# The low halves of the front's and the queries' weights: a vector subtraction against an adding transfer

## The chip, the cores and the metric

The kernel runs on one core of a Trainium2 chip. The metric is the time of one execution on the device in microseconds (us). The core has a matmul engine (PE, with its weight loads on PEld), a vector engine (DVE), a scalar engine (ACT), GpSimd (POOL) and SyncE (SP, which issues most transfers). All transfers run on 16 DMA engines. Every instruction stream is executed in order on its own engine; semaphores hold an instruction until what it needs has happened.

## The reference

One decoder layer over 1024 tokens with 1024 features:

```python
h = x @ w_in                                   # q | k | v | conv_a | conv_gate
att = sliding_window_attention(rotary(q), rotary(k), v, sinks)
cnv = silu(layer_norm(causal_conv31(conv_a * sigmoid(conv_gate))))
x = layer_norm(alpha * x + concat(att, cnv) @ w_out)
q = x @ w_query                                # 8 heads x 2 halves x 128
top = top16 of q @ sub_keys, then top16 of the 16 x 16 sums, per head
r = alpha * x + sum(gelu(x . u[ids]) * gates * v[ids])      # 128 experts a token
x = layer_norm(r + sigmoid(r @ w_gate) * (p @ w_ple))
```

All of it is float32. A float32 product is made here from three matmuls of rounded (fp32r) operands: high by high, high by low and low by high, where high is the operand rounded to fp32r and low is the operand less its high half.

## The kernel before

The 1024 tokens are cut into 8 tiles of 128: group A has three of them (384 tokens), group B five (640 tokens). The front runs for both groups: x is transposed and split, `s_conv` (streams c0, c1), `s_qkv` (q0, q1), the taps of the convolution (t0, t1, 31 vector instructions a channel block), attention (a0, a1), the convolution's norm (`s_cln`, in l0, l1), the output product `s_wout` (w0, w1), the first layer norm (n0, n1) and the expert queries `s_query` (y for A, and once more for B later). Then group A fetches its 768 rows of expert tables by indirect transfers (`s_gather`, line 775, issued by POOL), while group B does the same sums densely over the whole tables, which takes most of the time: `s_early` (products with u) and `s_dense` (products with v).

The weights of the front and of the queries come through one helper, `w_split` (lines 271 to 277). It is called 76 times, each time for 512 KB: 8 times each for c0 and c1, 6 each for q0 and q1, 8 each for w0 and w1, 16 for y and 16 for the queries of B. In `by_channel` (c, y and the queries) the piece is 1024 x 128, which lands as 8 runs of 512 bytes in each of the 128 partitions; in `by_token` it is 256 x 512 (runs of 2 KB: the last four of q, and w) or 512 x 256 (runs of 1 KB: the first two of q). Below such a call is a set. A set takes three pages, `wraw`, `wh` and `wl`, of a ring of six (`WPAGES`). SP loads `wraw` (line 273), ACT rounds it to `wh` (line 156, called from `split`), DVE subtracts and writes `wl` (line 152), and PE uses both in `mm3` (lines 160 to 162) until the set is done.

What sets the order: PE, ACT, DVE and SP get their order from a scheduler that lists the program on a simulated timeline. POOL alone keeps the order in which the program is written (line 201, `manual_schedule`). The program's order is that of `ORDER` (line 51), a list of streams with so many steps of each, and behind it the two lines that weave the queries of B with gathers:

```python
    weave((s_query(1), 16), (early, UQ), (rows, RQ))     # UQ 9, RQ 105
    weave((s_choose(1), 8 * nB), (early, UC), (rows, RC))  # UC 22, RC 45
```

So a step of the queries of B stands after every six or seven gathers. In the front POOL does the rotary products of attention (lines 370 to 375) and the low halves of the normed convolution (line 481, which is a `split` on POOL; it shows as line 152). In `ORDER` the second step of `s_cln` for group A stands just ahead of the first set of w0. The gathers have seven row buffers (`UB`), which DVE frees (lines 783 and 791), and `s_choose` takes its scratch from the same six pages as the sets.

Of the kernel before, what the change touches and what calls it, by code (L numbers as in the profile page):

```python
# [8 lines left out]
F32 = mybir.dt.float32  # L9
# [4 lines left out]
AF = mybir.ActivationFunctionType  # L14
OP = mybir.AluOpType
# [4 lines left out]
P = 128  # L20
# [78 lines left out]
def layer(tc, io):  # L99
    nc = tc.nc  # L100
# [49 lines left out]
    def sub(eng, o, a, b):  # L150

        return eng.tensor_tensor(o, a, b, op=OP.subtract)  # L152

    def split(hi, lo, src, eng):

        nc.scalar.copy(hi, src)  # L156
        return sub(eng, lo, src, hi.bitcast(F32))
# [30 lines left out]
    def wpage(shape, dt, name):  # L188
        return WP.tile(shape, dt, name=name, tag="wpage", bufs=WPAGES)
# [79 lines left out]
            split(dst[0][:, h:h + 4, sl], dst[1][:, h:h + 4, sl], ps.rearrange("p (k t) -> p k t", k=4), nc.vector)  # L269

    def w_split(src, k, n):
        raw = wpage([P, k, n], F32, "wraw")
        nc.sync.dma_start(raw, src.rearrange("(k p) n -> p k n", p=P))
        hi = wpage([P, k, n], F32R, "wh")
        lo = wpage([P, k, n], F32R, "wl")
        split(hi, lo, raw, nc.vector)
        return hi, lo

    def by_token(gi, src, c0, cn, sink_fn):

        g, (aH, aL) = groups[gi], act[gi]
        pss = [(ph() if j < 4 else pv())[:, :cn] for j in range(len(g))]
        kn = D // cn
        for kq in range(KD // kn):
            wh, wl = w_split(src[P * kn * kq:P * kn * (kq + 1), c0:c0 + cn], kn, cn)
            for j in range(len(g)):
                sl = slice(j * P, (j + 1) * P)
                for k in range(kn):
                    kk = kn * kq + k
                    mm3(pss[j], aH[:, kk, sl], aL[:, kk, sl], wh[:, k, :], wl[:, k, :], kk == 0, kk == KD - 1)  # L290
                if kk == KD - 1:
                    sink_fn(g[j], pss[j])
            yield

    def by_channel(gi, src, c0, sink_fn):

        aH, aL = act[gi]
        wh, wl = w_split(src[:, c0:c0 + P], KD, P)
        for (t0, tn) in n_split(len(groups[gi]) * P):
            ps = ph()[:, :tn]  # L300
            for k in range(KD):
                mm3(ps, wh[:, k, :], wl[:, k, :], aH[:, k, t0:t0 + tn], aL[:, k, t0:t0 + tn], k == 0, k == KD - 1)
            sink_fn(ps, t0, tn)
# [631 lines left out]
    n = len(outs) * len(sets)  # L935
# [115 lines left out]
```

## Time and profile before

| what | value |
|---|---|
| time, median of 3 runs | 2898.01 us (2894.17 to 2898.85) |
| the profiled execution's own time | 2893.7 us |
| its span, first to last instruction | 2891.9 us |
| mean granted clock of PE, share of full | 0.983 |
| PE, DVE, ACT, POOL busy, share of the span | 96%, 83%, 41%, 37% |

The profile is of one execution. "Busy" is the time in which an engine executes; issuing transfers is not counted. A line such as L152 can be that of a helper, so that the tile names tell the use: `wl<-wraw,wh` is the subtraction of `w_split`. An instruction's idle time before it is given with what ended it. The front of both groups takes about the first 500 us of the span, the queries of B run from about 600 to 850, and the dense part fills the rest.

### The profile page before, as it was taken

How to read it: one execution, taken by the hardware profiler on the slowest of the kernel's cores; microseconds unless marked ns; L12 is line 12 of the kernel's file. 1: busy time of each engine (PE TensorE's matmuls, PEld its weight loads, DVE VectorE, ACT ScalarE, POOL GpSimd, SP SyncE). 2: the span in 40 equal slices, each digit the busy share in tenths (PEclk: the TensorE clock that was granted, in tenths of full speed). 3: DMA queues.
4: the chain of work that ended last, by engine and by line, in shares of the span. 5: the costliest groups of instructions: out<-in, count | busy, mean ns of one | idle time of the engine just before them, and what ended most of it. 6: DMA issues, size and time to landing. Idle time of an engine off the chain costs nothing.

```text
span 2891.9 us, 47040 instructions
## 1 busy us (share of the span) xinstructions
PE 2788.4 (96%) x17619; PEld 2511.6 (87%) x17619; DVE 2397.7 (83%) x5137; ACT 1195.6 (41%) x2468; POOL 1071.4 (37%) x851
## 2 busy tenths in 40 slices
PE   8996899999999999999999999999999999999988
PEld 8974589999989999999999999777777777777788
DVE  7999768979999768777888876888888889888865
ACT  4455644533324466667565742222222222222143
POOL 0103010166671035543444443544444455444420
PEclk9997899999999999999999999999999999999999
DMA  5211343499994359998999898999999999999731
GB/s 157 79 52 41 100 122 108 169 379 323 350 326 169 122 218 373 347 347 332 344 330 357 335 359 312 346 339 344 329 353 345 348 365 339 352 348 337 253 108 46
DMA packets 322836, 774.14 MB, mean 268 GB/s; under 512 B 28945, under 2 KB 144145, under 8 KB 320048
## 3 DMA queue, kind: packets, MB, share of 16 engines
q0 software_dynamic: 110592, 402.70, 38.3%
q1 hardware_dynamic: 212016, 368.44, 36.1%
q8 instruction: 138, 2.26, 0.3%
q14 instruction: 90, 0.74, 0.1%
HBM read 681.78 MB, written 89.26 MB: 267 GB/s over the span
## 4 chain that ended last, share of the span: by engine, by line
PE 87%; DVE 9%; issue 1%; DMA 1%; ACT 1%; SPq 0%; POOL 0%; ACTq 0%; DVEq 0%
PE ph L160 15%; PE ph L161 15%; PE ph L162 15%; PE sum L160 7%; PE sum L161 7%; PE sum L162 6%; PE pv L756 4%; PE pt L661 4%; PE part L160 3%; PE part L162 3%; PE part L161 3%; DVE ag L791 1%; PE pt L674 1%; DVE cv L357 1%; DVE row L783 1%
## 5 line engine op out<-in xcount | busy, mean ns | idle before, releaser
L775 POOL DMA_INDIRECT row<-in_peer_v_dram,ids x384 | 513.1, 1336 | 705.6 <-DVE row L783 538.0
L775 POOL DMA_INDIRECT row<-in_peer_u_dram,ids x384 | 491.7, 1281 | 620.9 <-DVE ag L791 312.4
L160 PE MATMUL ph<-acth,uu 128*128 128x320 f32 x2048 | 651.6, 319 | 0.4 <-ACT uu L663 0.2
L161 PE MATMUL ph<-actl,uu 128*128 128x320 f32 x2048 | 636.7, 311 | 0.2 <-issue 0.2
L162 PE MATMUL ph<-acth,uu 128*128 128x320 f32 x2048 | 635.1, 311 | 0.0
L791 DVE SCALAR_TENSOR_TENSOR ag<-row,hb,ag 128x1024 f32<-128x1024 f32 x384 | 491.4, 1280 | 2.8 <-issue 1.3
L783 DVE SCALAR_TENSOR_TENSOR row<-row,x 128x1024 f32<-128x1024 f32 x384 | 466.8, 1219 | 6.6 <-DMA row<-in_peer_u_dram,ids 6.0
L161 PEld LDWEIGHTS ph<-actl,uu 128*128 128x128 f32 x2048 | 387.1, 189 | 1.2
L160 PEld LDWEIGHTS ph<-acth,uu 128*128 128x128 f32 x2048 | 386.4, 189 | 1.7 <-ACT uu L663 0.5
L162 PEld LDWEIGHTS ph<-acth,uu 128*128 128x128 f32 x2048 | 385.5, 189 | 1.0 <-issue 0.5
L161 PE MATMUL sum<-vl,ah 128*128 128x512 f32 x896 | 350.9, 398 | 0.0
L160 PE MATMUL sum<-vh,ah 128*128 128x512 f32 x896 | 337.0, 399 | 1.3 <-ACT vh L156 0.9
L156 ACT CAST ah<-ge 128x640 fp32r<-128x640 f32 x128 | 92.9, 728 | 562.1 <-DVE ge L870 336.5
L162 PE MATMUL sum<-vh,al 128*128 128x512 f32 x896 | 291.9, 396 | 0.0
L750 ACT ACTIVATE o<-oo,rest 128x128 bf16<-128x128 bf16 x640 | 196.7, 392 | 30.6 <-DVE oo L745 25.9
L160 PEld LDWEIGHTS sum<-vh,ah 128*128 128x128 f32 x896 | 169.6, 189 | 44.3 <-ACT vh L156 1.7
L161 PEld LDWEIGHTS sum<-vl,ah 128*128 128x128 f32 x896 | 169.6, 189 | 41.3
L162 PEld LDWEIGHTS sum<-vh,al 128*128 128x128 f32 x896 | 168.7, 188 | 41.2
L663 ACT CAST uu<-pt 128x512 fp32r<-128x512 f32 x256 | 150.8, 592 | 120.8 <-PE pt L661 111.5
L701 ACT ACTIVATE ge<-ph 128x320 f32<-128x320 f32 x256 | 108.7, 437 | 217.7 <-PE ph L162 183.7
L152 DVE TENSOR_TENSOR vl<-raw,vh 128x1024 fp32r<-128x1024 f32 x128 | 153.9, 1219 | 27.2 <-ACT vh L156 27.1
L160 PE MATMUL part<-vh,ah 128*128 128x512 f32 x384 | 155.0, 404 | 21.8 <-DVE acc L918 13.7
(300 smaller groups left out, 5592.6 us busy)
## 6 DMA issues: line engine op xcount, KB each, us to landing
raw<-in_peer_v_dram SPq DMA_DIRECT2D x128, 512.0 KB
raw<-in_peer_u_dram SPq DMA_DIRECT2D x81, 512.0 KB
g_dr<-stage SPq DMA_DIRECT2D x20, 2048.0 KB
gt<-g_dr SPq DMA_DIRECT2D x21, 1920.0 KB
e_dr<-ge SPq DMA_DIRECT2D x122, 320.0 KB
ge<-e_dr SPq DMA_DIRECT2D x122, 320.0 KB
uraw<-in_peer_u_dram SPq DMA_DIRECT2D x47, 512.0 KB
wraw<-in_peer_query_dram SPq DMA_DIRECT2D x32, 512.0 KB
```

What stands on the lines that cost most here:

```text
L152: return eng.tensor_tensor(o, a, b, op=OP.subtract)
L160: nc.tensor.matmul(ps, lh, rh, start=first, stop=False)
L161: nc.tensor.matmul(ps, lh, rl, start=False, stop=False)
L162: nc.tensor.matmul(ps, ll, rh, start=False, stop=last)
L661: nc.tensor.matmul(ps[:, k * P:(k + 1) * P], raws[c][:, (4 * h + k) * P:(4 * h + k + 1) * P], ident, is_transpose=True, start=k == 0, stop ...
L663: nc.scalar.copy(uu[:, 0], turned)
L701: nc.scalar.activation(ge[:, c0:c0 + cn], o, AF.Gelu)
L750: nc.scalar.mul(o2[:, 2, e], oo[:, 1, e], rest[:, t + e:t + e + 1])
L756: nc.tensor.matmul(ps[:, e * P:(e + 1) * P], o2[:, m, 4 * f4 + e], oo[:, 0, 4 * f4 + e], start=m == 0, stop=m == 2)
L775: nc.gpsimd.indirect_dma_start(out=t, out_offset=None, in_=table, in_offset=bass.IndirectOffsetOnAxis(ap=ids[i][:, s:s + 1], axis=0))
L783: behind(nc.vector.scalar_tensor_tensor(u, u, 1.0, x1, op0=OP.mult, op1=OP.mult, accum_out=hb[:, e:e + 1]), marks, TIE)
L791: behind(nc.vector.scalar_tensor_tensor(ag, v, blocks[b][:, e:e + 1], ag, op0=OP.mult, op1=OP.add), marks, TIE)
```

## The change

`w_split` no longer subtracts on DVE. ACT still rounds `wraw` to `wh`. ACT then writes the negative of `wh` to `wl`, and a transfer issued by POOL reads the weights from memory a second time and adds them onto `wl`. The three pages, the load by SP and the products stay as they are. `split` is used elsewhere as before.

```diff
     def w_split(src, k, n):
+        src = src.rearrange("(k p) n -> p k n", p=P)
         raw = wpage([P, k, n], F32, "wraw")
-        nc.sync.dma_start(raw, src.rearrange("(k p) n -> p k n", p=P))
+        nc.sync.dma_start(raw, src)
         hi = wpage([P, k, n], F32R, "wh")
         lo = wpage([P, k, n], F32R, "wl")
-        split(hi, lo, raw, nc.vector)
+        nc.scalar.copy(hi, raw)
+
+        nc.scalar.activation(lo, hi.bitcast(F32), AF.Copy, scale=-1.0)
+        nc.gpsimd.dma_start(lo, src, accum_op=OP.add)
         return hi, lo
```

## Rows read from the trace of the kernel before

**Rows 1.** The page, busy time and share of the span of each engine

```profile
PE 2788.4 (96%) x17619; PEld 2511.6 (87%) x17619; DVE 2397.7 (83%) x5137; ACT 1195.6 (41%) x2468; POOL 1071.4 (37%) x851
```

**Rows 2.** Stretches: busy us (count) of PE, PEld, DVE, ACT, POOL; clock, DMA share, GB/s

```profile
17.00:82.00 65.00, 65.00 (x378) 61.49 (x377) 57.19 (x102) 26.70 (x39) 1.06 (x2) 1.00 0.47 139
82.00:199.00 117.00, 117.00 (x774) 105.81 (x773) 112.46 (x193) 57.04 (x128) 15.43 (x23) 1.00 0.22 64
...
217.00:276.00 59.00, 34.94 (x186) 25.05 (x184) 59.00 (x85) 29.48 (x72) 23.47 (x28) 0.80 0.14 45
276.00:357.00 81.00, 67.23 (x321) 45.68 (x321) 60.20 (x112) 51.19 (x132) 0.00 (x0) 0.78 0.27 91
357.00:446.00 89.00, 89.00 (x444) 77.90 (x443) 56.64 (x190) 36.38 (x60) 7.26 (x8) 1.00 0.40 121
446.00:501.00 55.00, 53.04 (x333) 52.06 (x332) 52.73 (x183) 26.21 (x51) 0.00 (x0) 1.00 0.31 91
...
625.00:846.00 221.00, 212.82 (x1440) 208.26 (x1439) 209.71 (x639) 68.57 (x145) 152.73 (x106) 0.96 0.96 334
846.00:1000.00 154.00, 154.00 (x1075) 151.59 (x1075) 145.89 (x920) 70.36 (x133) 25.61 (x19) 1.00 0.49 178
```

**Rows 3.** Chain of waits between 199 and 357 us, its shares by line

```profile
by line: DVE cv L357 18.7%; PE pv L432 8.5%; PE pt L428 7.4%; PE pt L396 6.9%; PE ph L160 4.8%; PE ph L161 4.3%; PE ph L162 4.2%; DVE sc L400 4.2%; issue 3.7%; DMA xc<-in_x_dram 3.6%; DVE st L406 3.6%; PE pv L464 3.2%; DVE wl L152 2.9%; ACT
```

**Rows 4.** Stretches, tile `wl` alone: PE, PEld, DVE, POOL busy us (count)

```profile
82.00:217.00 135.00, 70.64 (x217) 40.71 (x216) 18.67 (x15) 0.00 (x0) 1.00 0.20 59
217.00:276.00 59.00, 9.43 (x20) 4.57 (x20) 4.96 (x4) 0.00 (x0) 0.80 0.14 45
```

**Rows 5.** Instructions by tile: count, duration min/median/max in ns, first and last start

```profile
L152 DVE TENSOR_TENSOR wl<-wraw,wh x76: 1199/1222/1876, 14.7 to 811.5; 128x1024 fp32r<-128x1024 f32 x76
...
L770 ACT ACTIVATE ag<-x x3: 1055/1073/1074, 504.6 to 2032.7; 128x1024 f32<-128x1024 f32 x3
```

**Rows 6.** Timeline: start us, duration us, engine, line; sets of c0

```profile
33.01 0.34 PE L162 MATMUL ph<-actah,wl 128*128 128x384 f32 x1
...
33.38 0.37 SPq L273 DMA_DIRECT2D wraw<-in_w_in_dram  x1
...
37.33 1.05 ACT L156 CAST wh<-wraw 128x1024 fp32r<-128x1024 f32 x1 [1.48 <-DMA wraw<-in_w_in_dram]
...
39.00 0.42 PE L162 MATMUL ph<-actah,wl 128*128 128x384 f32 x1
...
43.68 0.42 PE L162 MATMUL ph<-actah,wl 128*128 128x384 f32 x1
```

**Rows 7.** Timeline, sets of y: first use of `wl` in y6 and y15

```profile
446.40 0.34 PE L162 MATMUL ph<-actah,wl 128*128 128x384 f32 x1
...
494.72 0.34 PE L162 MATMUL ph<-actah,wl 128*128 128x384 f32 x1
```

**Rows 8.** Timeline of POOL: a short gather and a long one

```profile
558.29 0.94 POOL L775 DMA_INDIRECT row<-in_peer_u_dram,ids  x1 [0.30 <-issue]
...
668.15 3.08 POOL L775 DMA_INDIRECT row<-in_peer_v_dram,ids  x1 [0.30 <-DVE top L532]
```

**Rows 9.** First set of B's queries (SP's load, ACT's cast), and gathers before that load

```profile
594.70 0.39 SPq L273 DMA_DIRECT2D wraw<-in_peer_query_dram  x1
...
612.02 1.05 ACT L156 CAST wh<-wraw 128x1024 fp32r<-128x1024 f32 x1 [2.19 <-DMA wraw<-in_peer_query_dram]
...
556.00:594.70 38.70, 27.80 (x22) 1.00 0.93 346
```

**Rows 10.** Timeline: w0's first `wl` on PE, group A's norm on POOL

```profile
199.16 0.39 PE L161 MATMUL ph<-wl,actah 128*128 128x512 f32 x1
...
234.56 2.29 POOL L152 TENSOR_TENSOR actal<-cv,actah 128x384 fp32r<-128x384 f32 x2 [65.76 <-ACT actah L156]
```

## The prediction

> **What bounds the kernel now.** I read the busy shares first: PE 96%, DVE 83%, ACT 41%, POOL 37% [rows 1]. The share of PE over the whole span says only that most of it is bound by products; the 76 sets all lie before 850 us, so I read the stretches of that part next [rows 2]. Three kinds are to be seen. From 17 to 199 us PE is busy all the time, 65.0 of 65 and 117.0 of 117 us. From 217 to 276 DVE is busy for 59.0 of 59 us and PE for 34.9, at a clock of 0.80: there DVE sets the pace, and PE still idles to 357 (67.2 of 81). From 357 on PE is full again (89.0 of 89, 53.0 of 55, 212.8 of 221, 154 of 154). The chain of waits between 199 and 357 agrees: its largest share is DVE's taps, 18.7%, and the subtraction of `w_split` is on it by itself with 2.9% of 158 us, 4.6 us [rows 3]. So time that DVE is spared before 276 us can shorten the kernel; later PE would have to be given time, and a later low half takes it away.
>
> **What goes.** 76 subtractions of 1.22 us leave DVE [rows 5], 93 us in all. Only those ahead of the DVE-bound stretch or in it count: 15 between 82 and 217 (18.7 us) and 4 between 217 and 276 (5.0 us) [rows 4], together 23.7 us, since DVE is busy 112.5 of 117 us and then 59 of 59 there [rows 2]. I take them in full as -23.7; the other end is -4.6, what the chain itself holds. The first 14 lie in a stretch where PE is the bound, the rest behind 357 us.
>
> **What ACT gets.** 76 negations. A scaled copy of 128x1024 takes 1.07 us [rows 5]; ACT is busy 26.7 of 65 and 57.0 of 117 us in the dense stretches [rows 2], so the 1.07 us matters only as latency ahead of the transfer, in the sum below.
>
> **What the new transfer costs.** The low half now waits for ACT's negation, POOL's issue and a landing. No accumulating transfer is in this trace, so I bound the wait A from the negation's end to the landing. A plain load of a set takes 3.95 us from SP's issue (33.38) to the cast (37.33) [rows 6]. Between 446 and 501 us the 16 DMA engines move 91 GB/s at a share of 0.31, that is 294 GB/s when busy, so one pass over 512 KB is 1.8 us of all of them [rows 2]. An adding transfer reads `wl` too, and for the second operand I add one such pass: 3.95 + 1.8 = 5.75; with that read hidden it is 3.95. POOL's issue: the shortest gather, of 128 pieces, holds POOL for 0.94 us [rows 8]. If that price is fixed, A has 0.94; if it goes by pieces, a set of 1024 pieces has 8 x 0.94 = 7.5. Nothing shows which, and the row has a piece count and not a split of its time, so I take the middle in ratio, 2.65 (for sets of 2 KB runs with 256 pieces, 1.3). So A is 4.9 to 13.2 us, taken as 8.4 (by_channel) and 7.2 (the six sets of q0, two of them with 1 KB runs).
>
> **How the latency becomes time.** Six pages hold three sets in flight: SP issues a load (33.38) as soon as the third set before it has left PE (last matmul 33.01 + 0.34) [rows 6]. A set then needs 3.95 load + 1.05 cast + 1.07 negation + A + its own time on PE, 4.7 us (39.00 to 43.68) [rows 6], and three sets share that. Before, with 1.22 for DVE in place of 1.07 + A, it is (3.95 + 1.05 + 1.22 + 4.7) / 3 = 3.6, under the 4.7 that PE takes: hidden. After it is (10.8 + A) / 3.
> - c0, 8 sets: 19.2 / 3 = 6.4 against 4.7, +1.7 each, +13.6. q0, 6 sets: 18.0 / 3 = 6.0, +1.3 each, +7.8. Together +21.4 in a stretch where PE is the bound.
> - c1 and q1: 14 sets fill 117 us [rows 2], 8.4 each; (6.1 + 8.4 + 8.4) / 3 = 7.6 is less, so 0. PE is the cover; with A at 13.2 it would be +0.8 for each of the eight of c1.
> - w0: POOL keeps its written order, so its first low halves wait behind group A's norm, which ran on POOL at 234.6, though PE used the first one at 199.2 [rows 10]. About 9 us of product move from 199 to behind 240. PE idles 24 us between 217 and 276 [rows 2] and takes them: 0. The rotary products behind these issues wait too; attention waits for DVE there anyway.
> - w1 fills 357 to 446 with y0 to y5: (89 - 6 x 5.4) / 8 = 7.1 us a set; A for 2 KB runs is near 7.1, (6.1 + 7.1 + 7.1) / 3 = 6.8 is less: 0 for w1.
> - y: from y6 to y15 a set takes (494.72 - 446.40) / 9 = 5.4 us [rows 7]; after it is 6.4, +1.0 for 14 sets (y2 to y15), +14. PE is full from there to the end, so nothing gives it back.
>
> **The queries of B.** Here POOL's order costs most. The first low half stands behind three gathers and ahead of all others; its load was issued at 594.7 and cast at 612.0, and 22 gathers had been issued before 594.7 [rows 9]. Those now wait, and at each later step six or seven gathers wait for the set's negation, which waits for a page and so for PE. Their vector work, 22 x 1.2 us, moves back into a stretch where DVE is busy 209.7 of 221; the 16 subtractions that leave it give 19.5 us in return [rows 2, 5]. The DMA engines are at 0.96 there, and 16 adding transfers bring 16 x 3.6 = 58 us of their time; but gathers pushed behind 846 find a share of 0.49 and only 19 others [rows 2]. Ends: -8 (PE's idle time there goes) and +58; I take +10, near the lower end, since what is pushed out has room.
>
> **Sum:** -23.7 + 21.4 + 14 + 10 = +22 us. The profiled execution took 2893.7 (span 2891.9 and 1.8 around it); so 2916. The median of the runs is 4.3 above that execution, so I forecast 2920. A difference under 0.2% (5.8 us) can't be told from none by a measurement of this kernel.
>
> **Rivals.**
> 1. *The transfer is short and DVE's relief decides* (not slower). POOL's issue is a fixed 0.94 and the second read is hidden: A = 4.9. Then c0 and q0 cost (15.7 / 3 - 4.7) x 14 = +7, y nothing (5.2 under 5.4), the queries of B -8: -23.7 + 7 - 8 = -24, 2874. For it: sets are read by pieces as large as before, and SP's issue is 0.37 [rows 6]. Against it: the transfer reads twice. It decides where 14 x (2 x (10.8 + A) / 3 - 10.1) falls under 23.7, at A under 6.9.
> 2. *POOL pays by the piece.* A = 13.2 for 1024 pieces: c0 +26, q0 +10, c1 +7, y +37, the queries +45 (POOL gets 16 x 7.5 = 120 us beside 152.7 of 221 busy [rows 2]), -24: +101, 2999. For it: the pieces are eight times a gather's. Against it: a gather also reads an index for each piece.
> 3. *DVE's work lengthens POOL's issue.* Gathers take from 0.94 to 3.08 us, the long one begun while DVE was at L532 [rows 8]. If each issue pays those 2.1 us, 28 sets (c0, q0, y) cost 0.7 more each: +20 on the forecast, 2940. The Trainium skill, SBUF — State Buffer, section "SBUF: two separate sides", warns of this: descriptors for POOL's transfers are written through a port that some vector instructions hold. By that rule the change puts 76 transfers on the path that suffers; the spread of the gathers agrees, though it doesn't show the cause.
> 4. *The waits change places:* DVE's relief and PE's stalls cancel. With A near 6.9 the sum is within 5.8 us of nothing, 2898.
>
> That the change doesn't do what it says is no case: the subtraction is one instruction of DVE, and it is gone.
>
> **How the numbers follow.** Forecast 0.40 (2908 to 2935), rival 1 0.20, rival 2 0.13, rival 3 0.12, rival 4 0.15. Slower: 0.40 + 0.13 + 0.12 and a little of rival 4, 0.67. Faster: most of rival 1, 0.18. Same: 0.15. The range goes from just below rival 1 to just short of rival 2's full price, 2870 to 2990, which leaves out under 2 in 10.
>
> **What would show it.** In the profile after: DVE without L152 on `wl`; PE waiting for a DMA on `wl` in 17 to 82 and 446 to 501, with c0's sets at 6.4 us instead of 4.7; the 217 to 276 stretch shorter; POOL's rows for the new transfer near 2.7 us (0.94 speaks for rival 1, 7 for rival 2, a wide spread for rival 3); few gathers before the first set of B's queries. I am wrong if sets of c0 still take 4.7 us, or if the time before 357 us shrinks by more than the y sets and the queries of B give back.

## The result and the profile after

The changed kernel took 2961.49 us (median of 4 runs, 2959.06 to 2967.38) against 2896.09 us for the kernel before, a ratio of 1.0228 with a 95% interval of 1.0213 to 1.0243. That is 65 us slower, where +22 was forecast: the sign held, and the range (2870 to 2990) held the time, but the size was nearly three times the sum. The profiled execution took 2959.06 us with a span of 2957.3, against 2891.9 before, so it shows the same 65.4 us.

The page after has the busy times, the packets of POOL's queue (number, MB, share of 16 engines) and the shares of the chain that ended last; [rows 1] answer to the first line.

```profile
PE 2801.6 (95%) x17619; PEld 2517.6 (85%) x17619; DVE 2318.0 (78%) x5061; ACT 1268.1 (43%) x2543; POOL 1144.2 (39%) x927
...
q0 software_dynamic: 169152, 442.55, 47.2%
...
PE 68%; DMA 12%; DVE 11%; issue 6%; ACT 3%; POOL 1%; SPq 0%; DVEq 0%; POOLq 0%; ACTq 0%
```

The same lines of the page of before:

```profile
q0 software_dynamic: 110592, 402.70, 38.3%
...
PE 87%; DVE 9%; issue 1%; DMA 1%; ACT 1%; SPq 0%; POOL 0%; ACTq 0%; DVEq 0%
```

DVE has 79.7 us less to do (the 76 subtractions are 94 us; its other instructions took some 14 us more) and ACT 72.5 more. The chain tells the rest: transfers were 1% of it and are now 12%. POOL's queue took 0.472 x 2957.3 - 0.383 x 2891.9 = 288 us more of all 16 engines, 3.8 us for each of the 76 sets.

Stretches of the trace after (columns as in [rows 2], to which they answer; the marks are moved to the same sets):

```profile
17.00:117.00 100.00, 75.67 (x376) 67.14 (x377) 66.41 (x133) 42.07 (x55) 21.31 (x15) 0.88 0.88 168
117.00:248.00 131.00, 129.12 (x839) 112.69 (x838) 102.77 (x170) 77.37 (x164) 29.49 (x37) 1.00 0.59 114
248.00:310.00 62.00, 37.45 (x182) 27.72 (x180) 51.43 (x75) 34.89 (x72) 23.35 (x29) 0.78 0.53 110
310.00:392.00 82.00, 64.81 (x333) 43.43 (x333) 45.39 (x95) 55.98 (x141) 8.01 (x10) 0.85 0.46 110
392.00:495.00 103.00, 92.75 (x442) 79.48 (x443) 41.00 (x177) 48.69 (x73) 22.55 (x20) 0.97 0.73 158
495.00:567.00 72.00, 59.24 (x347) 56.59 (x346) 50.53 (x221) 37.62 (x65) 13.99 (x9) 0.93 0.87 155
...
687.00:912.00 225.00, 216.74 (x1494) 213.25 (x1493) 190.01 (x699) 81.36 (x164) 124.35 (x104) 0.98 1.04 324
```

The first stretch does in 100 us what took 65, the fifth in 72 what took 55, and in both the DMA engines are near full (0.88 and 0.87 where it was 0.47 and 0.31). What PE waits for in 0 to 117, 248 to 392 and 392 to 570 us (us in total, times, longest):

```profile
PE ph L161 <- DMA wl<-in_w_in_dram: 9.0, 2, 6.5
PE ph L162 <- DMA wl<-in_w_in_dram: 7.3, 4, 3.0
...
PE ph L161 <- DMA wl<-in_w_out_dram: 28.7, 5, 17.8
...
PE ph L162 <- DMA wl<-in_peer_query_dram: 14.9, 8, 5.1
```

To place the 65 us I cut both traces at the end of the last high-by-high product (line 160) of five sets, so that each stretch holds the same products. The forecast is the prediction's sum, sorted into the same stretches (its queries of B into the last but one).

| stretch, us | before | after | change | forecast |
|---|---|---|---|---|
| start to the first set of c0 | 22.8 | 32.1 | +9.3 | 0 |
| from there to the last set of q0 | 59.3 | 84.9 | +25.6 | +21.4 |
| to the first set of y (c1, q1, attention A, w0) | 278.3 | 279.1 | +0.8 | -23.7 |
| to the last set of y (w1 and y) | 139.8 | 171.1 | +31.3 | +14 |
| to the last set of B's queries | 345.8 | 344.5 | -1.3 | +10 |
| to the end | 2045.9 | 2045.6 | -0.3 | 0 |
| sum | 2891.9 | 2957.3 | +65.4 | +22 |

The new instructions, by tile (count, min/median/max in ns, first and last start; then the time from issue to landing in us):

```profile
L280 POOL DMA_DIRECT2D wl<-in_peer_query_dram x32: 1540/1622/1730, 338.2 to 888.8; - x32
L280 POOL DMA_DIRECT2D wl<-in_w_in_dram x28: 1187/1546/1827, 16.7 to 217.8; - x28
L280 POOL DMA_DIRECT2D wl<-in_w_out_dram x16: 1188/1203/1696, 262.4 to 479.1; - x16
...
L279 ACT ACTIVATE wl<-wh x76: 1039/1060/1093, 15.3 to 884.7; 128x1024 fp32r<-128x1024 f32 x76
...
DMA to landing us min/median/max: 5.9/7.4/16.3
```

### The profile page after: what moved, and what is told of

The parts are those of the page before. It is cut to its first block, busy times and chain, and to the rows that moved or that the text cites. A ratio compares the mean times of both kernels' runs of the same rounds, so it can differ in the third digit from the quotient of the medians.

```text
span 2957.3 us, 47285 instructions
## 1 busy us (share of the span) xinstructions
PE 2801.6 (95%) x17619; PEld 2517.6 (85%) x17619; DVE 2318.0 (78%) x5061; ACT 1268.1 (43%) x2543; POOL 1144.2 (39%) x927
## 4 chain that ended last, share of the span: by engine, by line
PE 68%; DMA 12%; DVE 11%; issue 6%; ACT 3%; POOL 1%; SPq 0%; DVEq 0%; POOLq 0%; ACTq 0%
PE ph L161 11%; PE ph L162 11%; PE ph L160 11%; PE sum L161 6%; PE sum L160 6%; PE sum L162 6%; PE pv L760 3%; PE pt L665 3%; PE part L160 3%; PE part L161 2%; PE part L162 2%; DVE ag L795 2%; DVE row L787 2%; DMA wl<-in_peer_query_dram 2%; DMA wraw<-in_w_in_dram 2%
## 5 line engine op out<-in xcount | busy, mean ns | idle before, releaser
L779 POOL DMA_INDIRECT row<-in_peer_v_dram,ids x384 | 495.5, 1290 | 628.2 <-DVE row L787 451.2
L779 POOL DMA_INDIRECT row<-in_peer_u_dram,ids x384 | 483.1, 1258 | 522.4 <-DVE ag L795 322.0
L160 PE MATMUL sum<-vh,ah 128*128 128x512 f32 x896 | 344.4, 399 | 1.3 <-ACT ah L156 1.3
```

Of the source, the lines that this page charges most:

```text
L160: nc.tensor.matmul(ps, lh, rh, start=first, stop=False)
L779: nc.gpsimd.indirect_dma_start(out=t, out_offset=None, in_=table, in_offset=bass.IndirectOffsetOnAxis(ap=ids[i][:, s:s + 1], axis=0))
```

## The experiments

Differences in us are medians less the median of the kernel before on the same chip; changes by stretch come from one profiled execution each. In the stretch behind the queries of B, in which `w_split` has no part, single executions lie between -4 and +12 us, also for a control whose median does not move (norm_dve_before, +8.5). I read nothing from that stretch.

**One part at a time.** `w_split` gets a flag; without it a set is made as before. Six kernels, each with another line for which sets are new:

```diff
+    def w_split(src, k, n, new):
         raw = wpage([P, k, n], F32, "wraw")
         ...
+        if not new:
+            split(hi, lo, raw, nc.vector)
+            return hi, lo
         nc.scalar.copy(hi, raw)
...
+    def adds(gi, src):
+        return src is w_in and gi == 0     # only_c0q0
```

In the others the line is `src is w_in and gi == 1` (only_c1q1), `src is w_out and gi == 0` (only_w0), `src is w_q and gi == 0` (only_y), `src is w_out and gi == 1` (only_w1) and `src is w_q and gi == 1` (only_qb).

> The adding transfer only for the 14 sets of group A's convolution and q, k, v (c0, q0); the other 62 sets subtract on DVE as before. Latency (the low half is late in a ring of six pages, and PE has no cover here): these sets end some 35 us later, as in the full change (117.2 against 82.3 us), and the total is 20 to 35 us over the kernel before. POOL's order (time is lost only where POOL's written order holds an issue): nothing stands ahead of these sets on POOL, so 0 to 3 us. Bytes (each second read slows the rest, 65 us / 76 sets = 0.86 us a set): 12 us.

> The adding transfer only for the 14 sets of c1 and q1, which PE consumes in 8 us each. Latency: hidden, and DVE is spared 14 x 1.22 = 17 us ahead of the stretch that it bounds, so 5 to 17 us under the kernel before. POOL's order: the rotary products stand behind some of these issues, 0 to 5 us over. Bytes: 12 us over.

> The adding transfer only for the eight sets of group A's output product (w0). POOL's order: the first issue waits behind the low halves of group A's norm, PE stands still for it as in the full change (17.8 us), 10 to 18 us over the kernel before. Latency alone: eight sets at about 1 us more, partly in PE's idle time, 0 to 6 us. Bytes: 7 us.

> The adding transfer only for the 16 sets of group A's queries (y). Latency: y6 to y15 go from 5.4 to 6.9 us a set, and with y2 to y5 the total is 18 to 25 us over the kernel before. POOL's order: nothing long stands ahead of them on POOL, 0 to 5 us. Bytes: 14 us.

> The adding transfer only for the eight sets of w1. As predicted: 0. As the full change's trace reads (w1's end moves 6.6 us more than the end of y5): 3 to 10 us over the kernel before.

> The adding transfer only for the 16 sets of the queries of B, between the gathers. As predicted: +10 us (POOL's order holds gathers, the DMA engines are full). As the full change's trace reads (from the first to the last set 217.6 us against 214.0 before, and 6 us won back behind): within 6 us of the kernel before.

Measured, with the change of each stretch of the table above:

| kernel | ratio (95%) | us | first set | c0, q0 | to y | w1, y | to B's last |
|---|---|---|---|---|---|---|---|
| only_c0q0 | 1.0101 (1.0084 to 1.0119) | +27 | +10.2 | +26.2 | -6.3 | -0.9 | -0.8 |
| only_c1q1 | 1.0037 (1.0023 to 1.0051) | +8 | -0.3 | 0.0 | +2.9 | -0.4 | +0.7 |
| only_w0 | 1.0078 (1.0058 to 1.0098) | +22 | +0.7 | 0.0 | +22.7 | -0.2 | +1.6 |
| only_y | 1.0104 (1.0084 to 1.0124) | +27 | -0.2 | 0.0 | +0.8 | +21.0 | -1.1 |
| only_w1 | 1.0034 (1.0023 to 1.0046) | +11 | +0.9 | +0.1 | +3.6 | +12.3 | +3.2 |
| only_qb | 1.0002 (0.9991 to 1.0014) | 0 | +0.9 | 0.0 | +3.1 | -0.6 | -0.2 |

The losses of the whole change are reproduced where they arise: the first set and c0/q0 by the first kernel (+36.4, and +34.9 in the whole change), the stretch of w1 and y by two (21.0 + 12.3, and +31.3). Only the stretch to y doesn't add up: the five parts have +24 there, the whole +0.8. What PE waits for, in only_w0 between 199 and 360 us and in only_y between 360 and 525:

```profile
PE ph L161 <- DMA wl<-in_w_out_dram: 35.6, 4, 21.7
```

```profile
PE ph L162 <- DMA wl<-in_peer_query_dram: 12.5, 7, 3.6
```

What follows: c0/q0, w0, y and w1 each cost by themselves; the queries of B cost nothing by themselves, though I had put +10 on them; c1 and q1 cost little on their path (PE waited 3.8 us for their `wl`) but returned none of the vector time that they save (+8, where 5 to 17 us less was expected if DVE's relief counts).

**What DVE's relief is worth.** The negation stays, the transfer goes; the low half is then only the negative of the high half.

```diff
         nc.scalar.activation(lo, hi.bitcast(F32), AF.Copy, scale=-1.0)
-        nc.gpsimd.dma_start(lo, src, accum_op=OP.add)
```

> All 76 sets are rounded and negated by ACT as in the change, and no transfer follows: the weights are not added, so the low half is the negative of the high one. It has all of DVE's relief and ACT's added work and none of the transfer. If DVE's relief was worth what the prediction said, 20 to 24 us under the kernel before; if DVE's time was not what held the stretch from 217 to 357 us, within 6 us of the kernel before, and the whole loss of the change is then the transfer's.

Measured: 0.9885 (0.9866 to 0.9904), -33 us, more than the 20 to 24 expected. By stretch -0.1, +4.1, -23.3, -1.8 and -17.7. Its windows of c1 and q1, and where [rows 2] have 34.94 of 59 and 67.23 of 81 for PE:

```profile
86.00:215.00 129.00, 129.00 (x839) 113.03 (x838) 114.07 (x193) 79.10 (x166) 23.30 (x24) 1.00 0.21 62
...
217.00:276.00 59.00, 50.83 (x247) 35.19 (x245) 54.98 (x87) 41.76 (x96) 21.78 (x28) 0.83 0.19 63
276.00:357.00 81.00, 70.80 (x376) 53.32 (x376) 48.41 (x128) 61.19 (x139) 3.41 (x4) 0.89 0.32 103
```

PE does 50.8 us of work where it did 34.9. So the relief of all 76 sets is worth 23.3 us ahead of y, the size that the prediction took, and another 17.7 in the stretch with the queries of B, where it had at most 8. The transfer itself then costs 33 + 65 = 98 us.

That the 23.3 come from the 19 subtractions which the prediction counted is not shown. 13 of them are those of c1 and q1 and 6 those of w0. only_c1q1 takes the 13 away: the last tap of the convolution then ends at 291.8 us in place of 307.7, yet w0's last low product starts at 314.8, as late as before (312.2); in relief_all it starts at 293.9. PE's wait for the cast of a set of w0 goes the same way (from 199 us to 360 in before, to 363 in only_c1q1, to 341 in relief_all):

```profile
PE ph L160 <- ACT wh L156: 9.1, 2, 8.6
...
PE ph L160 <- ACT wh L156: 8.2, 1, 8.2
...
PE ph L160 <- ACT wh L277: 0.2, 1, 0.2
```

So w0's own subtractions are the likelier place; no run takes them alone away without a transfer.

**Which part of the transfer.** Two kernels keep every instruction and every wait; like relief_all they don't compute the reference. The first adds only the first slab of a set (64 KB of a 1024 x 128 piece, 128 or 256 KB of the others); the second moves all of it but overwrites.

```diff
-        nc.gpsimd.dma_start(lo, src, accum_op=OP.add)
+        nc.gpsimd.dma_start(lo[:, :1, :], src[:, :1, :], accum_op=OP.add)   # small_add
+        nc.gpsimd.dma_start(lo, src)                                        # plain_pool
```

> The change, with the adding transfer for the first slab of each set alone (an eighth of the bytes for by_channel, a quarter or half for by_token), so the other slabs hold the negative of the high half. Issue, completion, POOL's order and every wait stay; the transfer's time on the DMA engines nearly goes. If the engines' time sets the pace: 2864 (all transfers gone) and w0's wait of at most 18 us, so 2866 to 2884. If fixed latency in the ring sets it (landing still 5 to 6 us): (10.8 + 5.5) / 3 = 5.4 us a set of the first 14 against 4.55, +12, y within 2 us, so 2884 to 2900.

> The change with a transfer on POOL that writes the weights over the negated half instead of adding them, so the low half holds the weights themselves; the same bytes are read from memory, nothing is read from the page. If the adding makes the transfer slow, its landing falls from 7.4 us to some 5.5 and the total by (1.9 / 3) x 28 = 18 us and w0's share; if issue, fetch and completion are the most of it, landing and total stay within 1 us and 6 us.

Measured: small_add 0.9978 (0.9963 to 0.9992), -5 us; plain_pool 1.0041 (1.0027 to 1.0055), +12 us. By tile, small_add's issues and landings, and plain_pool's issues:

```profile
L280 POOL DMA_DIRECT2D wl<-in_peer_query_dram x32: 853/928/1025, 301.6 to 816.1; - x32
...
DMA to landing us min/median/max: 2.5/4.1/10.0
```

```profile
L280 POOL DMA_DIRECT2D wl<-in_peer_query_dram x32: 876/927/952, 309.6 to 835.3; - x32
L280 POOL DMA_DIRECT2D wl<-in_w_in_dram x28: 698/876/1076, 17.0 to 200.1; - x28
L280 POOL DMA_DIRECT2D wl<-in_w_out_dram x16: 698/716/757, 244.9 to 441.1; - x16
```

The 98 us fall into three steps: -33 without a transfer, -5 with a short one (28 us for POOL's order, its issue, a short landing and an eighth to a half of the bytes), +12 with the whole 512 KB (17 us for bytes), +65 with the adding (53 us, far more than the 18 us and w0's share that were expected of it). About half of the price is the adding: it lengthens the issue from 0.93 to 1.62 us for 1024 pieces and the time on the DMA engines. Queues by packets, MB and share of 16 engines: after in 17 to 117 us, plain_pool in 17 to 100, before in 17 to 82:

```profile
q0 software_dynamic: 11295, 7.77, 57.1%
q1 hardware_dynamic: 11796, 8.98, 30.3%
```

```profile
q0 software_dynamic: 10652, 7.44, 44.9%
```

```profile
q1 hardware_dynamic: 11777, 8.96, 46.5%
```

An adding set of 0.524 MB takes 57.1 us x 0.524 / 7.77 = 3.85 us of all engines, an overwriting one 0.449 x 83 x 0.524 / 7.44 = 2.62, and SP's load of the same bytes 0.465 x 65 x 0.524 / 8.96 = 1.77. These windows hold pieces of 512 bytes to 2 KB. Over the whole run POOL's queue moves the same packets and bytes when it overwrites, at a share of 0.452 of 2908.0 us:

```profile
q0 software_dynamic: 169152, 442.55, 45.2%
```

That is 207 us over before, 2.7 us a set against 3.8 with the adding. For y alone, all of it in pieces of 512 bytes, an adding set takes 0.575 x 67 x 0.524 / 4.73 = 4.3 us (500 to 567 us of after) and an overwriting one 0.537 x 61 x 0.524 / 4.98 = 3.4 (455 to 516 us of plain_pool). So the adding costs 1.2 to 1.5 overwriting transfers of POOL and in c0 and q0 2.2 of SP's loads. The Trainium skill, Collectives: The Full Stack, section "The bandwidth ceiling: the fold count and why AG ≠ RS ≠ AR", puts the price of the add in a collective down to its two source reads; carried over to this transfer, which is an estimate, that would give about 2. That lies between the two; the runs don't show which base is fair, since POOL's overwriting transfer also turns float32 into fp32r and SP's load does not.

**How many sets are in flight.** One page more (with one taken from another ring, so that it fits) or one less, with the change and without it:

```diff
-PAGES, WPAGES, RAWS, GEB, OB = 5, 6, 3, 3, 2
+PAGES, WPAGES, RAWS, GEB, OB = 4, 7, 3, 3, 2     # ring7, ring7_before
+PAGES, WPAGES, RAWS, GEB, OB = 5, 5, 3, 3, 2     # ring5, ring5_before
```

> The change with seven pages for the sets instead of six, the room taken from the other ring (four pages instead of five). Latency: 3.5 sets in flight instead of three, so a set of c0 or y takes (10.8 + 7.4) / 3.5 = 5.2 us instead of 6.1 or more, some 25 us off the change's 2961 if the smaller ring costs nothing. POOL's order and bytes: no gain.

> The kernel before with seven pages for the sets and four in the other ring, the control of that step. Latency: the sets of before are hidden with six pages, so nothing is gained, 0 to 10 us over the kernel before for the smaller other ring; the gain of the seventh page is then the change's alone. If it gains some 30 us here too, the ring and not the transfer's latency was what the step showed.

> The change with five pages for the sets instead of six. Latency: 2.5 sets in flight instead of three, (10.8 + 7.4) / 2.5 = 7.3 us a set of c0, q0 and y against 6.5, 20 to 35 us over the change's 2961. Engines' time: the pace is held by 6.1 us a set whatever the ring, within 8 us of 2961.

> The kernel before with five pages, the control of that step. Latency: 10.9 / 2.5 = 4.4 us a set is still under PE's 4.55 to 4.7, so 0 to 10 us over the kernel before.

| pages | with the change | without | what the change costs | c0/q0, us a set with the change |
|---|---|---|---|---|
| 7 | 1.0103 (1.0081 to 1.0126), +32 | 1.0042 (1.0026 to 1.0058), +12 | 20 | 72.3 / 13 = 5.56 |
| 6 | 1.0228 (1.0213 to 1.0243), +65 | the kernel before | 65 | 84.9 / 13 = 6.53 |
| 5 | 1.0358 (1.0340 to 1.0375), +107 | 1.0093 (1.0075 to 1.0111), +31 | 76 | 97.1 / 13 = 7.47 |

The last column follows the sets in flight. In the changed kernel a set needs its page for `wraw` only until the cast, so two pages a set count. In the trace after the sixth load of c0 is issued at 46.6 us, when the third set before it has left PE (46.7), and its last low product ends at 66.8: three sets share these 20.2 us, 6.7 each. The landings between 17 and 117 us (the last number, median in us):

```profile
wl<-in_w_in_dram POOLq DMA_DIRECT2D x15, 512.0 KB, 6.8
wraw<-in_w_in_dram SPq DMA_DIRECT2D x14, 512.0 KB, 5.4
```

With 5.4 for `wraw`, 1.05 cast, 1.06 negation, 0.3 to POOL's issue, 6.8 from there to the landing of `wl` and 4.7 on PE, a set takes 19.3 us; over 3.5, 3 and 2.5 sets in flight that is 5.5, 6.4 and 7.7, against 5.56, 6.53 and 7.47. The landings are those of six pages. With each run's own (4.2 and 6.6 us with seven pages, 4.0 and 6.5 with five) the sums are 5.1 and 7.0: the order holds, the size to half a us. The kernel before lost 6.9 us to the fifth page there (66.2 for the 13 sets, 5.1 each in place of 4.56), where its sum had none. So in c0 and q0 latency through the pages decides. The seventh page ends the gain, since the DMA engines are then full, at a share of 0.97 in ring7, and 3.85 + 1.77 = 5.6 us of them for a set are what was measured:

```profile
17.00:104.00 87.00, 71.15 (x371) 63.80 (x371) 65.30 (x132) 40.50 (x53) 21.52 (x15) 0.94 0.97 192
```

The control with five pages cost more than expected, +31, part of it in w1 and y (+11.9). So the whole change does not follow the page count as well as this one stretch: from six to five it lost only 11 us more than its control.

**w0 behind the norm.** The trace after, POOL and then PE (start, duration, and the idle time before with what ended it):

```profile
257.75 4.68 POOL L152 TENSOR_TENSOR actal<-cv,actah 128x384 fp32r<-128x384 f32 x4 [38.35 <-ACT actah L156]
262.38 2.42 POOL L280 DMA_DIRECT2D wl<-in_w_out_dram  x2
```

```profile
268.53 0.79 PE L161 MATMUL ph<-wl,actah 128*128 128x512 f32 x1 [17.78 <-DMA wl<-in_w_out_dram]
```

POOL stands for 38 us at group A's norm, the first two transfers of w0 are issued behind it, and PE stands 17.8 us. Then the norm's low halves of group A were moved to DVE, with the change and without it:

```diff
-                split(aH[:, 4 + b, sl], aL[:, 4 + b, sl], c[:, b, sl], nc.gpsimd)
+                split(aH[:, 4 + b, sl], aL[:, 4 + b, sl], c[:, b, sl], nc.gpsimd if gi else nc.vector)
```

> The change, with the low halves of group A's normed convolution (four instructions) on DVE instead of POOL, so that nothing long stands ahead of w0's first issue on POOL. POOL's order: the wait of 17.8 us for w0's first low half goes and the total falls by 10 to 20 us, to some 2943 to 2952. Latency (w0's delay lies in parallel with that of the first 14 sets): 0 to 6 us off.

> The kernel before with the same move of four instructions from POOL to DVE, as the control of that step. 0 to 5 us from the kernel before by either theory: 4 x 0.5 us more on DVE.

Measured: 1.0189 (1.0171 to 1.0207) and 0.9995 (0.9985 to 1.0005): +56 us with the change, -2 without. PE's wait on these transfers between 248 and 392 us falls from 28.7 to 11.1 us, the longest from 17.8 to 2.9:

```profile
PE ph L161 <- DMA wl<-in_w_out_dram: 11.1, 5, 2.9
```

The stretch to y is 11.4 us shorter than with the change as it was (-10.6 in place of +0.8), of which 6.0 are lost again in w1 and y. So the hold behind the norm is real, and is worth about 10 us in the end (+56 against +65).

**The subtraction on POOL instead.** For the 52 sets of c, q, y and w1 `split` runs on POOL with no second transfer:

```diff
-        split(hi, lo, raw, nc.vector)
+        split(hi, lo, raw, nc.gpsimd)
```

> No transfer: the subtraction itself runs on POOL instead of DVE for 52 sets (all but w0 and the queries of B). DVE gets its relief in the front, and the low half comes some 2.3 us after the cast instead of 1.2 (128x2560 takes 5.7 us on POOL). If latency is what costs, the sets still hide it ((3.95 + 1.05 + 2.3 + 4.7) / 3 = 4.0 under 4.7) and the total is 8 to 20 us under the kernel before; if POOL's order or a share of the port with DVE costs more, 0 to 15 us over.

Measured: 1.0168 (1.0147 to 1.0189), +49 us, outside both expectations; c0 and q0 have +37.8 of it, and there PE waited 25.4 us for two subtractions. By tile, and on the timeline of POOL, DVE and PE:

```profile
L152 POOL TENSOR_TENSOR wl<-wraw,wh x55: 2352/2414/18417, 14.5 to 2842.7; 128x1024 fp32r<-128x1024 f32 x52, 128x2560 fp32r<-128x2560 f32 x3
```

```profile
69.43 18.42 POOL L152 TENSOR_TENSOR wl<-wraw,wh 128x1024 fp32r<-128x1024 f32 x1 [4.25 <-PE ph L162]
...
94.25 15.88 POOL L152 TENSOR_TENSOR wl<-wraw,wh 128x1024 fp32r<-128x1024 f32 x1 [2.62 <-issue]
```

```profile
66.53 19.13 DVE L364 SCALAR_TENSOR_TENSOR cv<-hc,cw,cv 128x384 f32<-128x384 f32 x36
...
91.98 15.95 DVE L364 SCALAR_TENSOR_TENSOR cv<-hc,cw,cv 128x384 f32<-128x384 f32 x30
```

```profile
87.90 0.80 PE L161 MATMUL ph<-wl,actah 128*128 128x512 f32 x1 [13.99 <-POOL wl L152]
```

A subtraction takes 2.4 us on POOL, but the two that met an unbroken run of DVE's taps (36 and 30 of them) ended only some 2 us after it. It is no way out here. Of the versions that compute the reference none is measurably faster than the kernel before.

## Why the prediction was wrong, and what of it held

The forecast of +22 had the direction and missed the size at three terms of its sum. The stretch with w0 was to give back 23.7 us, with w0's late low halves at 0, and gave +0.8. w1 at 0 and y at +14 came to +31.3. The first set, at 0, cost 9.3. Against that the queries of B cost 11 less than forecast.

**What bounds each stretch: right.** PE's full stretches at 17 to 82 and 446 to 501 us [rows 2] were where a later low half became time, and six pages were the means. The forecast of 6.4 and 6.0 us a set for c0 and q0 averages 6.2; measured 6.53. A was taken as 8.4 us and 0.3 + 6.8 = 7.1 was measured; in return `wraw` took 5.4 us to land beside the adding transfers, where [rows 6] gave 3.95. The two misses nearly cancel, which is luck; the term stands (+21.4 against +25.6).

**The first set: a term that was not in the sum, +9.3.** The sum counted sets in a steady row, three in flight. No earlier set covers the first: its transfer was issued at 16.7 and its first low product ran at 27.5.

**w0 at nothing: the step that failed worst.** The text saw that w0's first low halves would stand behind the norm [rows 10], but let PE's 24 idle us of 217 to 276 take the 9 us of product. PE takes its instructions in order, so idle time that lies behind a waiting matmul can't be filled with it or with anything after it. The stall of 17.8 us on PE and 28.7 in all falls into just the stretch in which DVE's relief should have appeared; by itself w0 costs 22.7 us there (only_w0). So the relief, -23.7 in the sum and 23.3 in relief_all, does not show: DVE idles there instead (51.4 of 62 us busy, where [rows 2] has 59.0 of 59). The match of 23.7 and 23.3 may be luck, since 13 of the 19 subtractions behind it gave nothing in only_c1q1. Here the prediction named the wait, but not what stands behind it on PE.

**c1 and q1 at nothing: about right.** PE is busy 129.1 of the 131 us between 117 and 248 us after the change. Their last set ends later because work from behind has moved ahead of it: in relief_all, without any transfer, the stretch holds 129 us of PE in 129, and 839 products as here, where [rows 2] has 774. But the relief that was counted for these sets did not come: only_c1q1 had its taps done 16 us earlier and was still +2.9 us at y. Its path there runs through w0, as read above; what holds w0 stays open.

**w1 at nothing and y at +14: too low, +31.3 in the trace.** Cut once more, the 31.3 are 7.3 for y1 to y5, 6.6 for w1, 7.0 from w1's last set to y6 and 10.4 for y7 to y15. The 7.0 belong to y6: only_y, where w1 is as before, has 5.1 there, and only_w1 has 0. So y's sets cost 24.7 us, 1.6 each in place of +1.0 (y7 to y15 take 60.5 / 9 = 6.7 us each, and 5.6 before between the same marks). Why they take more than the 6.4 of the sum stays open. The granted clock in 495 to 567 us is 0.93 where it was 1.00, but it can hardly be the main cause: only_y loses 8.6 us in y7 to y15, against the 10.4, at 0.97.

```profile
454.00:522.00 68.00, 57.34 (x345) 54.52 (x344) 50.65 (x223) 36.47 (x63) 14.00 (x9) 0.97 0.87 159
```

The 6.6 of w1 were counted at nothing; alone it costs 12.3. There the cover was 0.3 us a set (6.8 against 7.1), from a mean that took in work that is not w1's: before, its sets follow each other every 6.8 us, so there was none.

**The DMA engines: sized, but set against nothing.** The prediction had 16 x 3.6 us for the transfers of B's queries, and 3.85 a set was measured. It did not set the 3.6 beside PE's time in the front: with 1.8 for the load that is 5.4 us of all engines for a set that PE does in 4.6. Six pages hid this floor, since latency asked for more; seven pages ran into it.

**The queries of B at +10: wrong, 0.** Alone they cost nothing (0.9991 to 1.0014). The gathers did move (the first from 556.5 to 616.7 us), but the stretch has 216.7 of 225 us of PE as before, and what the transfer costs there is about what DVE's relief brings (17.7 us without the transfer, 1.3 with it). The vector work that moves back leaves DVE at 190 of 225 us, under the 209.7 of 221 of before [rows 2], and did not stand in PE's way.

**The rivals.** Rival 1 (a fixed issue, a hidden read) is out with a landing of 7.4 us, though the issue is nearly fixed: 1.20 us for 256 pieces, 1.62 for 1024, not the 7.5 of rival 2. Rival 3, 2.1 us more an issue, is out. The issues of y and, with DVE busy 190 of 225 us, of B's queries:

```profile
L280 POOL DMA_DIRECT2D wl<-in_peer_query_dram x16: 1540/1549/1567, 338.2 to 556.1; - x16
...
L280 POOL DMA_DIRECT2D wl<-in_peer_query_dram x16: 1676/1695/1730, 646.5 to 888.8; - x16
```

They differ by 0.15 us. So the warning of the Trainium skill, SBUF — State Buffer, section "SBUF: two separate sides", drawn on there, is not borne out by these issues. Rival 4's point, A near 6.9, was almost met by the measured 7.1, and yet the sum is +65, because w0, w1 and the first set were counted at nothing and y too low.

Shown by experiments: the pages and the latency in c0 and q0, the hold of w0, the share of the adding, the value of the relief of all sets, the free queries of B. Only argued: that in the stretch to y the late c0 and q0 and w0's stall use up the same idle time, which would be why the parts have +24 there and the whole +0.8. Open: which subtractions make the relief, and what y's sets take beyond the sum.

## What to carry to other kernels

Before a step is moved from an engine to a transfer, divide its whole chain (load, cast, issue, landing, use) by the sets in flight, set that beside the consumer's time for a set, and set the DMA engines' time for a set beside it as well; then add the first set, which nothing covers. Idle time of an engine that works in order only hides work if it lies ahead of the instruction that waits. And a queue that keeps the written order passes a wait on to all behind it: look there first for what will stand at its head.

## What the hardware showed

- An adding transfer of 512 KB takes 3.85 us of the 16 engines in c0 and q0 (4.3 in y, in 512-byte pieces), 2.2 times SP's plain load and 1.2 to 1.5 times an overwriting one from POOL's queue. POOL issues it in 1.62 us in place of 0.93 for 1024 pieces.
- PE that waits often is also busy longer with the same products: 75.7 us in place of 65.0 in the first stretch. Its granted clock there is 0.88, a mean of its two levels (1.2 and 2.4 GHz), where it was 1.00; but plain_pool has 73.0 us at 1.00, so most of the difference is not the clock's.

```profile
17.00:100.00 83.00, 73.00 (x376) 63.93 (x376) 64.22 (x131) 41.39 (x54) 12.48 (x15) 1.00 0.83 201
```

- POOL's two-input subtraction stood for 18.42 us beside a run of 36 taps of DVE, 19.13 us, in place of 2.4, and a second one for 15.88 us beside 30 taps, 15.95 us. The Trainium skill, SBUF — State Buffer, section "Who interferes with whom", says that a vector instruction with two inputs in that memory contends with a GpSimd one that reads it; the run agrees, and shows that the wait can last as long as DVE's run.
